# An RWKV-7 chunk scan: the outputs' score part multiplied by the inverse ahead of the scan, and the solve added into the output's bank

## The chip, the cores and the metric

The kernel runs on one core of a Trainium2 chip. Its metric is the device time of one execution in microseconds, the median over the runs shown. TensorE (PE) multiplies matrices, its weight loads are shown as an engine of their own (PEld); VectorE (DVE), ScalarE (ACT) and GpSimd (POOL) do the rest, and SyncE (SP) issues the transfers.

## The reference, cut to what matters

Two layers. Each normalizes x, projects it with one matrix, and feeds three mixers (pooling over windows, retention, RWKV-7); their gated outputs are projected, merged with sigmoid gates and projected once more. D_MODEL is 1024, the sequence 1024, a branch 512 wide. The change is in the third mixer, 8 heads of 64:

```python
def rwkv7_time_mix(p, shift_mu, w0, w2, a0, a2, k_k, k_a, r_k, ln_w, ln_b):
    ...
    xs = tuple(jnp.moveaxis(z, 1, 0) for z in (r_h, w_h, k_h, v_h, -kk, kk * a_h))

    def step(S, inp):
        r_t, w_t, k_t, v_t, a_t, b_t = inp
        sa = jnp.einsum('bhvk,bhk->bhv', S, a_t)
        S = (S * w_t[:, :, None, :] + sa[..., None] * b_t[:, :, None, :]
             + v_t[..., None] * k_t[:, :, None, :])
        return S, jnp.einsum('bhvk,bhk->bhv', S, r_t)

    _, y = lax.scan(step, jnp.zeros((B, H, N, N), jnp.float32), xs)
    y = jnp.moveaxis(y, 0, 1)
    y = head_norm(y, RWKV_NORM_EPS).reshape(B, T, BRANCH_W) * ln_w + ln_b
    ...
```

## The kernel before, in words

**Projections.** The large products run as three products of fp32r parts (`hi` by `hi`, `hi` by `lo`, `lo` by `hi`), 128x128 weights by 512 columns, into the banks `acc`. The weights come as `wr`; the scalar engine makes the high part `wh`, GpSimd the low part `wl`.

**RWKV by chunks.** The 1024 steps are 16 chunks of 64; two heads of 64 share the 128 partitions, so there are four head pairs (`hp`) a layer, one `rwkv_task` each, one after the other. A task prepares, for all 16 chunks, `AR` (decayed a and r), `BK` (decayed b and k), its transpose `BKt`, and the masked scores: the product burst `g` (64 rows by 128 columns, two heads in the two row halves) gives the triangular matrices that land in `Z` (a against b), `GQ` (r against b) and `KG` (both against k).

**The solve.** In a chunk, sa solves a triangular system; the kernel inverts the 64x64 unit triangular matrix of each chunk and head. The vector engine inverts the diagonal 32x32 blocks in `M` (a part of the tile `VB`) by 30 pairs of operations, and transposes move blocks between `Z`, `VB` and `G` (`STREAM_TRANSPOSE`). The 32x32 block below the diagonal takes two bursts of small products, `m1` and `m2` (both are named `m` in the profile), each 32 products of 32x32, four corners of the array in turn; the scalar and the vector engine empty their four banks (`mt<-m`, `G<-m`; the tiles `mn` and `mt` are W1 and W2). Then the whole inverse stands in `GQ` (columns 0 to 63), put together with two copies `G<-Z`.

**The scan.** For each chunk `c`, before the change, TensorE issues five products, each in float32 (two passes, so two MATMUL records): `cy<-VB,G` (values by scores, for the next chunk ahead of time, `own_values`), `cy<-S,AR` (state), `ch<-xst,G` (the inverse, applied to the right-hand side in `xst`), `ch<-Z,BKt` (the state update) and `cy<-xst,G` (the scores of the outputs, applied to the solution). Between them the vector engine copies the right-hand side into `xst` and the solution into `Z`, the scalar engine copies the solution into `xst`, and two operations make the new state `S`. Rows 64 to 127 of `cy` are the chunk's outputs, copied to `y`. The last chunk has no state update.

**Order.** The program is recorded first. `lanes` hold generators (tasks); each `yield` gives a delay on a virtual clock, and `pump` advances those that are due between projection products, so that tasks are woven into the projections. `plan_layer` says which weight tile comes next; while the RWKV tasks last it moves gate tiles ahead (written with `gd<-gsg`, read back with `gs<-gd`). Then `needs` finds the dependences, `cost` prices each instruction, and `weave` orders the instructions of each engine by a simulation with these prices: at each step the operation that can begin first, and among equals the one recorded with the earlier time. `bursts` are lists of products that wait together and run back to back. Each engine executes its list in order, so a wait holds up everything behind it. PSUM has three `acc` banks, two `mx`, two `cy` and one `ch`; bursts use `mx`, `cy`, `ch`, `cy`.

The planner's prices that the change or the prediction speaks of, before it:

```python
                o.load, o.occ, o.dur = (55, 53, 272) if k == 64 else (15, 15, 191)
...
            elif w == "transpose":
                d = 100 + 1.82 * n
...
            else:
                d, o.lock = 150 + 0.53 * n, True
```

The second is a transpose of the vector engine and the last its copy within SBUF, in ns for n columns; `lock` means that it holds a port that GpSimd's operations with `lock` also want.

Of the kernel before, what the change touches and what calls it, by code (L numbers as in the profile page):

```python
# [18 lines left out]
P = 128  # L19
# [241 lines left out]
class Prog:  # L261
# [50 lines left out]
    def needs(self):  # L312
# [6 lines left out]
        for chain in self.chains.values():  # L319
            old = []  # L320
            for b in chain:
                w, r, mine = [], [], []
                for o, m, write in uses[b]:
                    free = True
                    for q, x in w:
                        if x & m and q is not o:
                            o.pred[q.i] = "d"
                            free = False
                    if not write:
                        r.append((o, m))  # L330
# [12 lines left out]
                old = mine  # L343
# [10 lines left out]
    def cost(self, o):  # L354
# [6 lines left out]
        if o.eng == "PE":  # L361
            n = o.outs[0].free_size()
            rhs = o.ins[1]
            k = rhs.index.shape[0] * 32
            o.twice = rhs.dtype != F32R and w != "transpose"
            o.rows = k
            if rhs.dtype == F32R:
                o.load, o.occ, o.dur = (107, (n + 32) / 2.4, n / 2.4 + 176) if k == 128 else (55, 116, 393)
            elif k == 128:
                o.load, o.occ, o.dur = 109, 53, 273 if n > 1 else 250  # L370
            else:
                o.load, o.occ, o.dur = (55, 53, 272) if k == 64 else (15, 15, 191)
# [4 lines left out]
        if o.eng == "DVE":  # L377
            if w == "reciprocal":
                d = 140 + 6.2 * n
            elif w == "transpose":  # L380
                d = 100 + 1.82 * n
            elif w == "tensor_tensor_scan":
                d, o.lock = 150 + 1.7 * n, True
            elif w == "tensor_reduce":
# [29 lines left out]
    def weave(self):  # L414
# [25 lines left out]
        while len(order) < len(ops):  # L440
# [124 lines left out]
def trunk_kernel(ctx, tc, xT, cvec, pos, vecs, consts, w_ada, w_all, pool_w, lora_w, out):  # L565
# [47 lines left out]
    def cyt(s):  # L613
        return ps_c.tile([P, HF], F32, tag="cy", name=nm(s))
# [607 lines left out]
    def rwkv_task(l, hp, kT, rT, vp, lt, lw):  # L1222
# [169 lines left out]
        for i, (rows, hd, c8) in enumerate(quad[1:]):  # L1392
            (nc.scalar.copy, nc.vector.tensor_copy)[i % 2](
                q4(W1, rows, 1), GQ[0:32, c8, 32 * hd : 32 * hd + 32]
            )
        for b in (1, 0):
# [4 lines left out]
        for i, (rows, hd, c8) in enumerate(quad):  # L1401
            if i != 1:
                nc.scalar.copy(q4(W2, rows, 1), Z[32:64, c8, 64 * hd + 32 : 64 * hd + 64])
        place_values(1)

        def quads(name, lhsT, rhs):
            pss = [mx(name), cyt(name), cht(name), cyt(name)]
            at = len(nc.ops)
            for v in range(8):
                for g, (rows, hd, c8) in enumerate(quad):  # L1410
                    u, o = 2 * (c8.start + v) + hd, slice(32 * v, 32 * v + 32)
                    mmul(pss[g][rows, o], lhsT(g, rows, u, o), rhs(g, rows, u, o))
            nc.bursts.append((at, len(nc.ops)))
            return pss

        half2 = lambda t, rows, o: t[rows, 256 + o.start : 256 + o.stop]
        yield 1000
        yield wait(W1, G)
        pss = quads(
            "m1",  # L1420
            lambda g, rows, u, o: W1[rows, o] if g else N_[0:32, u, 32:64],
            lambda g, rows, u, o: half2(W1, rows, o) if g else t1(rows, u),
        )
# [6 lines left out]
        pss = quads(  # L1430
            "m2",
            lambda g, rows, u, o: W2[rows, o],
            lambda g, rows, u, o: half2(W2, rows, o) if g != 1 else N_[32:64, u, 32:64],
        )
        for g, (rows, hd, c8) in enumerate(quad):
            (nc.scalar.copy, nc.vector.tensor_copy)[g % 2](
                GQ[64 * hd : 64 * hd + 32, c8, 32:64], q4(pss[g], rows)
            )
        SS = [sp.tile([P, P], F32, tag="S", name=nm("S"), bufs=2) for _ in range(2)]
        for S in SS:  # L1440
            nc.gpsimd.memset(S, 0.0)
# [9 lines left out]
        for c in range(16):  # L1451
# [13 lines left out]
            if c < 15:  # L1465
                cy_next = own_values(c + 1)
            yield wait(xst)
            ch = cht("ch")
            mmul(ch[:, 0:P], GQ[:, c, :], xst)
            nc.vector.tensor_copy(Z[0:64, c, :], ch[0:64, 0:P])  # L1470
            for hd in range(2):
                cols = slice(64 * hd, 64 * hd + 64)
                nc.scalar.copy(xst[cols, cols], Z[0:64, c, cols])
            yield wait(Zt)
            if c < 15:
                mmul(ch[:, P : 2 * P], BKt[:, c, :], Z[:, c, :])
                for hd in range(2):
                    rw = slice(64 * hd, 64 * hd + 64)
                    cols = slice(P + 64 * hd, P + 64 * hd + 64)
                    if c:  # L1480
                        nc.vector.scalar_tensor_tensor(
                            Sn[rw, rw], ch[rw, cols], pc[rw, c : c + 1], SP[rw, rw], op0=ALU.mult, op1=ALU.add
                        )
                    else:
                        nc.vector.tensor_scalar_mul(Sn[rw, rw], ch[rw, cols], pc[rw, c : c + 1])
# [400 lines left out]
    for l in range(L):  # L1886
# [297 lines left out]
```

## Time and profile before

| what | value |
|---|---|
| median of 3 runs | 2299.82 us (2298.17 to 2301.0) |
| the profiled execution's own time | 2299.37 us |
| its span | 2297.6 us |
| mean granted clock of TensorE | 0.996 |
| busy: PE, DVE, ACT, POOL | 2249.1, 1470.3, 871.7, 821.2 us |
| products `acc<-hhi,wh`, `acc<-hlo,wh`, `acc<-hhi,wl` | 2000 each |

In the groups of instructions a row reads: line, engine, operation, what is written from what, shapes, count, then busy us and the mean ns of one, then the idle time of the engine just before them and what ended it. Every instruction has the same line (561), since one function issues them all; they are told apart by their tiles. In the timeline a row is start, duration (both us), engine and so on; `x32` means that many in a row, and a bracket holds the idle time before it with what ended that. Products are pipelined, so the difference of two starts, and not a duration, says how much of TensorE's time one takes. A row of stretches has from and to, the length, the busy time of TensorE with its count, the granted clock, the share of the transfer engines and GB/s.

### The profile page before, as it was taken

The page shows a single profiled execution, that of the slowest core. Times are in us where ns is not written, and L with a number is a line of the kernel's source. Part 1 is how long each engine was busy: PE and PEld are TensorE (multiplying, and loading weights), DVE is VectorE, ACT ScalarE, POOL GpSimd, SP SyncE. Part 2 cuts the span into 40 slices and gives each one's busy share as a digit, 9 for nine tenths or more (in the row PEclk, how much of TensorE's full clock was granted, in tenths as well). Part 3 has the DMA queues.
Part 4 walks back from the last instruction along what each step waited for, and adds up shares of the span by engine and source line. Part 5 has one row for each costly group of instructions (what it writes and reads, how often), then busy time and mean ns, then how long its engine had stood idle before and what let it go on. Part 6 is the DMA issues. An engine that isn't in the chain of part 4 may idle for free. (4 is left out here: it accounts for less than half of the span.)

```text
span 2297.6 us, 33901 instructions
## 1 busy us (share of the span) xinstructions
PE 2249.1 (98%) x12520; PEld 1879.9 (82%) x12520; DVE 1470.3 (64%) x2866; ACT 871.7 (38%) x1770; POOL 821.2 (36%) x714
## 2 busy tenths in 40 slices
PE   5999999999999999999999999999999999999998
PEld 4888888888888788887888888888878888788888
DVE  8677478587678754668547847866875784313644
ACT  5643442433443342223443334344344434212343
POOL 5222333233333342463442233323324333326441
PEclk9999999999999999999999999999999999999999
DMA  8132113112232225767431211311211222535442
GB/s 286 33 121 79 42 42 98 42 42 76 62 91 75 89 86 178 234 207 229 138 94 59 74 42 42 98 38 42 89 51 42 70 92 64 181 109 161 124 143 83
DMA packets 125942, 226.75 MB, mean 99 GB/s; under 512 B 14288, under 2 KB 17616, under 8 KB 125776
## 3 DMA queue, kind: packets, MB, share of 16 engines
q1 hardware_dynamic: 125776, 224.59, 31.7%
q8 instruction: 98, 1.61, 0.3%
q14 instruction: 68, 0.56, 0.1%
HBM read 176.03 MB, written 48.50 MB: 98 GB/s over the span
## 5 line engine op out<-in xcount | busy, mean ns | idle before, releaser
L561 POOL TENSOR_TENSOR wl<-wr,wh 128x512 fp32r<-128x512 f32 x342 | 458.2, 1340 | 1007.3 <-ACT wh L561 976.8
L561 PE MATMUL acc<-hhi,wh 128*128 128x512 f32 x2000 | 805.6, 403 | 0.8 <-DVE r L561 0.7
L561 PE MATMUL acc<-hlo,wh 128*128 128x512 f32 x2000 | 805.2, 403 | 0.0
L561 PE MATMUL acc<-hhi,wl 128*128 128x512 f32 x2000 | 801.6, 401 | 0.0
L561 ACT CAST wh<-wr 128x512 fp32r<-128x512 f32 x342 | 212.0, 620 | 621.6 <-PE acc L561 439.7
L561 PEld LDWEIGHTS acc<-hhi,wh 128*128 128x128 f32 x2000 | 377.5, 189 | 66.4 <-DVE r L561 1.4
L561 PEld LDWEIGHTS acc<-hlo,wh 128*128 128x128 f32 x2000 | 377.6, 189 | 64.2 <-issue 2.1
L561 PEld LDWEIGHTS acc<-hhi,wl 128*128 128x128 f32 x2000 | 377.5, 189 | 63.1
L561 PE MATMUL acc<-oG,wh 128*128 128x512 f32 x384 | 149.8, 390 | 0.0
L561 PE MATMUL acc<-oG,wl 128*128 128x512 f32 x384 | 149.7, 390 | 0.0
L561 PE MATMUL acc<-olo,wh 128*128 128x512 f32 x384 | 149.7, 390 | 0.0
L561 ACT COPY xst<-Z 64x64 f32<-64x64 f32 x256 | 62.4, 244 | 136.1 <-DVE Z L561 133.0
L561 DVE TENSOR_TENSOR VB<-VB,tm 64x30 f32<-64x30 f32 (+14 forms) x240 | 107.1, 446 | 7.0
L561 DVE SCALAR_TENSOR_TENSOR S<-ch,pc,SP 64x64 f32<-64x64 f32 x224 | 63.4, 283 | 68.9 <-PE ch L561 59.9
L561 DVE TENSOR_TENSOR tm<-VB 64x30 f32<-64x30 f32 (+14 forms) x240 | 97.6, 407 | 7.1
L561 DVE COPY xst<-cy 64x64 f32<-64x64 f32 x256 | 55.5, 217 | 72.7 <-PE cy L561 45.6
L561 DVE COPY Z<-ch 64x128 f32<-64x128 f32 x128 | 36.1, 282 | 92.4 <-PE ch L561 92.0
L561 ACT ACTIVATE gsg<-acc 128x512 f32<-128x512 f32 x86 | 51.2, 596 | 93.1 <-PE acc L561 63.0
L561 PEld LDWEIGHTS acc<-oG,wl 128*128 128x128 f32 x384 | 72.1, 188 | 15.0
L561 PEld LDWEIGHTS acc<-oG,wh 128*128 128x128 f32 x384 | 72.1, 188 | 14.9
L561 PEld LDWEIGHTS acc<-olo,wh 128*128 128x128 f32 x384 | 72.1, 188 | 14.8
L561 DVE SCALAR_TENSOR_TENSOR mrg<-gs,acc 128x512 f32<-128x512 f32 x32 | 21.9, 686 | 93.0 <-PE acc L561 93.0
(280 smaller groups left out, 3738.9 us busy)
## 6 DMA issues: line engine op xcount, KB each, us to landing
wr<-in_w_all SPq DMA_DIRECT2D x364, 256.0 KB, 2.7
gd<-gsg SPq DMA_DIRECT2D x86, 256.0 KB, 2.0
gs<-gd SPq DMA_DIRECT2D x86, 256.0 KB, 2.8
wada<-in_w_ada SPq DMA_DIRECT2D x70, 256.0 KB, 3.3
ol<-od SPq DMA_DIRECT2D x64, 256.0 KB, 3.6
ringG<-in_w_ada SPq DMA_DIRECT2D x26, 256.0 KB, 4.9
x<-in_xT SPq DMA_DIRECT2D x16, 256.0 KB, 5.0
od<-po SPq DMA_DIRECT2D x16, 256.0 KB, 2.1
```

The source lines that it names most:

```text
L561: f(*[put(x) for x in o.args], **{k: put(x) for k, x in o.kw.items()})
```

## The change

Ahead of the scan, the score matrix of the outputs is multiplied by the inverse for each chunk and head (burst `qt`, 32 products of 64x64 by 64 columns); the result takes the place of the scores in `GQ` (columns 64 to 127). To have the factor the right way round, `m2` is computed in both orders (the second half with the operands exchanged), another transpose `T2` of the diagonal blocks is made, and the blocks are laid out once for `qt` and once, less the identity, for the scan. The inverse less the identity is added to what already stands in the bank `cy`: one product `cy<-xst,G` now gives the solution (rows 0 to 63) and the finished outputs (rows 64 to 127). The product into `ch` with the inverse, and the scalar engine's copies of the solution into `xst`, are gone; `ch` is used for the state update alone.

Beside it: the planner's price of transposes (two values, by the number of dimensions of the output) and of small products; an order between readers of one PSUM buffer on different engines; a rule in `weave` that lets a ready GpSimd operation go first where a vector operation wants the same port within 50 ns; a fifth `mo` buffer; and the `post` tasks are drained with `rwkv` and `mix` before the branches are merged.

```diff
@@ needs
                     if not write:
+                        if b.space == PSUM:
+                            for q, x in r:
+                                if q.eng != o.eng:
+                                    o.pred.setdefault(q.i, "a")
                         r.append((o, m))
@@ cost
-                o.load, o.occ, o.dur = (55, 53, 272) if k == 64 else (15, 15, 191)
+                quad = k == 32 or o.ins[0].free_size() == 64
+                o.load, o.occ, o.dur = (15, 15, 191 if k == 32 else 230) if quad else (55, 53, 272)
...
-                d = 100 + 1.82 * n
+                d = (100 if len(o.outs[0].index.shape) == 3 else 300) + 1.88 * n
@@ weave
+            s = begin(o, f, lk)
+            if e == "DVE" and o.lock and ready["POOL"]:
+                g = free["POOL"]
+                lim = min(begin(x, g, 0.0) for x in ready["POOL"]) + 1e-6
+                x = min((x for x in ready["POOL"] if begin(x, g, 0.0) <= lim), key=lambda x: (x.prio, x.i))
+                if x.lock and lim < s + 50:
+                    o, e, q = x, "POOL", ready["POOL"]
+                    s = begin(o, g, lock["DVE"] - 100)
             q.remove(o)
-            s = begin(o, f, lk)
@@ trunk_kernel
-    t_mo = slot("mo", 4, HF + 16)
+    t_mo = slot("mo", 5, HF + 16)
...
-        drain("rwkv", "mix")
+        drain("rwkv", "mix", "post")
@@ rwkv_task, the solve
+        nc.vector.tensor_copy(q4(W1, quad[1][0], 1), GQ[0:32, 8:16, 0:32])
+        nc.scalar.copy(GQ[64:96, :, 0:32], GQ[0:32, :, 32:64])
+        nc.scalar.copy(q4(W1, quad[3][0], 1), GQ[0:32, 8:16, 32:64])
+        for rows in (slice(64, 96), slice(0, 32)):
+            nc.gpsimd.memset(GQ[rows, :, 32:64], 0.0)
...
+        T2 = VBt[32:64, 1024:2048]
+        nc.vector.transpose(
+            out=T2.rearrange("p (a b s) -> p s a b", s=32, b=2),
+            in_=M[32:64, :].rearrange("p (a b s) -> p s a b", s=32, b=2),
+        )
+        T2 = T2.rearrange("p (a b s) -> p a b s", s=32, b=2)
+        for hd in range(2):
+            nc.scalar.copy(GQ[64 * hd + 32 : 64 * hd + 64, :, 32:64], T2[:, :, hd, :])
+        back(0)
...
-        nc.scalar.copy(GQ[64:128, :, 0:64], Z[0:64, :, 64:128])
-        nc.vector.tensor_copy(GQ[0:64, :, 0:64], Z[0:64, :, 0:64])
...
+        for swap in range(2):
+            for g, rows, hd, c, o in units:
+                x, t2 = W2[rows, o], half2(W2, rows, o) if g != 1 else N_[32:64, 2 * c + hd, 32:64]
+                if swap:
+                    mmul(pss[g][rows, o], x, t2)
+                else:
+                    mmul(half2(pss[g], rows, o), t2, x)
+        nc.bursts.append((at, len(nc.ops)))
         for g, (rows, hd, c8) in enumerate(quad):
             (nc.scalar.copy, nc.vector.tensor_copy)[g % 2](
-                GQ[64 * hd : 64 * hd + 32, c8, 32:64], q4(pss[g], rows)
+                GQ[64 * hd + 32 : 64 * hd + 64, c8, 0:32], q4(pss[g], rows, 1)
             )
+        for g, (rows, hd, c8) in enumerate(quad):
+            (nc.scalar.copy, nc.vector.tensor_copy)[g % 2](
+                Z[0:32, c8, 64 * hd + 32 : 64 * hd + 64], q4(pss[g], rows)
+            )
+        yield 800
+        yield wait(G)
+        pss = [cht("qt"), cyt("qt")]
+        at = len(nc.ops)
+        for k in range(8):
+            for e in range(2):
+                for hd in range(2):
+                    rows = slice(64 * hd, 64 * hd + 64)
+                    mmul(
+                        pss[hd][64 * e : 64 * e + 64, 64 * k : 64 * k + 64],
+                        GQ[rows, 2 * k + e, 0:64], GQ[rows, 2 * k + e, 64:128],
+                    )
+        nc.bursts.append((at, len(nc.ops)))
+        eye = ident[0:64, 0:64].unsqueeze(1).to_broadcast([64, 16, 64])
+        for hd in range(2):
+            rows = slice(64 * hd, 64 * hd + 64)
+            nc.vector.tensor_tensor(GQ[rows, :, 0:64], Z[0:64, :, rows], eye, op=ALU.subtract)
+            for e in range(2):
+                nc.scalar.copy(
+                    GQ[rows, e:16:2, 64:128],
+                    pss[hd][64 * e : 64 * e + 64, :].rearrange("p (c n) -> p c n", n=64),
+                )
@@ rwkv_task, the scan
-            ch = cht("ch")
-            mmul(ch[:, 0:P], GQ[:, c, :], xst)
-            nc.vector.tensor_copy(Z[0:64, c, :], ch[0:64, 0:P])
-            for hd in range(2):
-                cols = slice(64 * hd, 64 * hd + 64)
-                nc.scalar.copy(xst[cols, cols], Z[0:64, c, cols])
-            yield wait(Zt)
+            mmul(cy[:, 0:P], GQ[:, c, :], xst, start=False, skip_group_check=True)
             if c < 15:
-                mmul(ch[:, P : 2 * P], BKt[:, c, :], Z[:, c, :])
+                nc.vector.tensor_copy(Z[0:64, c, :], cy[0:64, 0:P])
+            o = (c % 8) // 2 * P
+            nc.scalar.copy(y[64 * par : 64 * par + 64, o : o + P], cy[64:128, 0:P])
+            if c < 15:
+                yield wait(Zt)
+                ch = cht("ch")
+                mmul(ch[:, 0:P], BKt[:, c, :], Z[:, c, :])
...
-            yield wait(xst)
-            mmul(cy[:, 0:P], GQ[:, c, :], xst, start=False, skip_group_check=True)
-            o = (c % 8) // 2 * P
-            nc.scalar.copy(y[64 * par : 64 * par + 64, o : o + P], cy[64:128, 0:P])
             yield wait(Sn)
```

More of the change, by code (lines that the diff above doesn't have):

```diff
@@ L1391, in rwkv_task, with back @@
         )
[L1392 to L1396, printed above, removed]
+        nc.vector.tensor_copy(q4(W1, quad[1][0], 1), GQ[0:32, 8:16, 0:32])
[3 more added lines that the diff above has]
+            nc.gpsimd.memset(GQ[rows, :, 32:64], 0.0)
+        def back(b):
             q = slice(32 * b, 32 * b + 32)
@@ L1400, in rwkv_task @@
             )
-        for i, (rows, hd, c8) in enumerate(quad):
-            if i != 1:
+        back(1)
+        for rows, hd, c8 in quad:
+            if rows.start != 32:
                 nc.scalar.copy(q4(W2, rows, 1), Z[32:64, c8, 64 * hd + 32 : 64 * hd + 64])
-        place_values(1)
[L1406 to L1414, printed above, removed]
+        T2 = VBt[32:64, 1024:2048]
@@ L1416, in rwkv_task @@
+        nc.vector.transpose(
[6 more added lines that the diff above has]
+        back(0)
+        place_values(1)
         half2 = lambda t, rows, o: t[rows, 256 + o.start : 256 + o.stop]
+        units = [
+            (g, rows, hd, c8.start + v, slice(32 * v, 32 * v + 32))
+            for v in range(8) for g, (rows, hd, c8) in enumerate(quad)
+        ]
@@ L1417, in rwkv_task @@
         yield 1000
         yield wait(W1, G)
[L1419 to L1423, printed above, removed]
+        pss = [mx("m1"), cyt("m1"), cht("m1"), cyt("m1")]
+        at = len(nc.ops)
+        for g, rows, hd, c, o in units:
+            mmul(
+                pss[g][rows, o],
+                W1[rows, o] if g else N_[0:32, 2 * c + hd, 32:64],
+                half2(W1, rows, o) if g % 2 else GQ[rows, c, 0:32],
+            )
@@ L1424, in rwkv_task @@
+        nc.bursts.append((at, len(nc.ops)))
         for g, (rows, hd, c8) in enumerate(quad):
             (nc.scalar.copy, nc.vector.tensor_copy)[g % 2](W2[rows, 0:256], pss[g][rows, 0:256])
-        nc.scalar.copy(GQ[64:128, :, 0:64], Z[0:64, :, 64:128])
-        nc.vector.tensor_copy(GQ[0:64, :, 0:64], Z[0:64, :, 0:64])
         yield 800
         yield wait(W2)
[L1430 to L1434, printed above, removed]
+        pss = [mx("m2"), cyt("m2"), cht("m2"), cyt("m2")]
@@ L1435, in rwkv_task @@
+        at = len(nc.ops)
+        for swap in range(2):
+            for g, rows, hd, c, o in units:
+                x, t2 = W2[rows, o], half2(W2, rows, o) if g != 1 else N_[32:64, 2 * c + hd, 32:64]
[4 more added lines that the diff above has]
+        nc.bursts.append((at, len(nc.ops)))
         for g, (rows, hd, c8) in enumerate(quad):
             (nc.scalar.copy, nc.vector.tensor_copy)[g % 2](
-                GQ[64 * hd : 64 * hd + 32, c8, 32:64], q4(pss[g], rows)
+                GQ[64 * hd + 32 : 64 * hd + 64, c8, 0:32], q4(pss[g], rows, 1)
@@ L1438, in rwkv_task @@
             )
+        for g, (rows, hd, c8) in enumerate(quad):
[5 more added lines that the diff above has]
+        pss = [cht("qt"), cyt("qt")]
+        at = len(nc.ops)
+        for k in range(8):
+            for e in range(2):
+                for hd in range(2):
+                    rows = slice(64 * hd, 64 * hd + 64)
+                    mmul(
+                        pss[hd][64 * e : 64 * e + 64, 64 * k : 64 * k + 64],
+                        GQ[rows, 2 * k + e, 0:64], GQ[rows, 2 * k + e, 64:128],
+                    )
@@ new lines, in rwkv_task @@
+        nc.bursts.append((at, len(nc.ops)))
+        eye = ident[0:64, 0:64].unsqueeze(1).to_broadcast([64, 16, 64])
[6 more added lines that the diff above has]
+                    pss[hd][64 * e : 64 * e + 64, :].rearrange("p (c n) -> p c n", n=64),
+                )
@@ L1467, in rwkv_task @@
             yield wait(xst)
-            ch = cht("ch")
-            mmul(ch[:, 0:P], GQ[:, c, :], xst)
-            nc.vector.tensor_copy(Z[0:64, c, :], ch[0:64, 0:P])
-            for hd in range(2):
-                cols = slice(64 * hd, 64 * hd + 64)
-                nc.scalar.copy(xst[cols, cols], Z[0:64, c, cols])
-            yield wait(Zt)
-            if c < 15:
-                mmul(ch[:, P : 2 * P], BKt[:, c, :], Z[:, c, :])
+            mmul(cy[:, 0:P], GQ[:, c, :], xst, start=False, skip_group_check=True)
+            if c < 15:
+                nc.vector.tensor_copy(Z[0:64, c, :], cy[0:64, 0:P])
[5 more added lines that the diff above has]
+                mmul(ch[:, 0:P], BKt[:, c, :], Z[:, c, :])
                 for hd in range(2):
                     rw = slice(64 * hd, 64 * hd + 64)
-                    cols = slice(P + 64 * hd, P + 64 * hd + 64)
                     if c:
                         nc.vector.scalar_tensor_tensor(
-                            Sn[rw, rw], ch[rw, cols], pc[rw, c : c + 1], SP[rw, rw], op0=ALU.mult, op1=ALU.add
+                            Sn[rw, rw], ch[rw, rw], pc[rw, c : c + 1], SP[rw, rw], op0=ALU.mult, op1=ALU.add
                         )
                     else:
-                        nc.vector.tensor_scalar_mul(Sn[rw, rw], ch[rw, cols], pc[rw, c : c + 1])
+                        nc.vector.tensor_scalar_mul(Sn[rw, rw], ch[rw, rw], pc[rw, c : c + 1])
             yield 500
-            yield wait(xst)
-            mmul(cy[:, 0:P], GQ[:, c, :], xst, start=False, skip_group_check=True)
-            o = (c % 8) // 2 * P
-            nc.scalar.copy(y[64 * par : 64 * par + 64, o : o + P], cy[64:128, 0:P])
             yield wait(Sn)
```

## The prediction

> **What bounds the kernel now.** I read the page's shares and slices first, then the waits of TensorE's queue, then the timeline of TensorE inside one scan, one small burst and one wide burst. The profiled execution took 2299.37 us, 0.45 under the median of 2299.82; its span is 2297.6, so 1.8 us lie around it. The sums below are made in that execution and put on the median.
>
> ```profile
> span 2297.6 us, 33901 instructions
> PE 2249.1 (98%) x12520; PEld 1879.9 (82%) x12520; DVE 1470.3 (64%) x2866; ACT 871.7 (38%) x1770; POOL 821.2 (36%) x714
> PE   5999999999999999999999999999999999999998
> PEclk9999999999999999999999999999999999999999
> ...
> PE acc L561 <- DVE sq L561: 20.1, 3, 12.0
> PE cy L561 <- DVE G L561: 4.3, 3, 2.3
> ...
> PE rkv L561 <- ACT rkt L561: 2.5, 1, 2.5
> ...
> PE m L561 <- DVE mn L561: 1.4, 2, 0.7
> ```
>
> TensorE is busy in every slice but the first, at full clock; of its few waits 20.1 us belong to the start. Everything else has air (the vector engine 36%, the scalar engine 62%). So a product taken out of TensorE's queue moves the end by its whole place in that queue, and one put in costs its whole place. What a product takes is not its duration, since they are pipelined: it is read from starts.
>
> **The product removed.** Each chunk step of the scan now issues five products, the last of them `cy<-xst`, the second one with the matrix GQ and the state xst. The change folds it into the first.
>
> ```profile
> L561 PE MATMUL cy<-xst,G 128*128 128x128 f32 x256 | 49.3, 274 | 0.0
> ...
> 239.70 0.39 PE L561 MATMUL acc<-hhi,wh 128*128 128x512 f32 x1
> 239.93 0.39 PE L561 MATMUL acc<-hlo,wh 128*128 128x512 f32 x1
> 240.16 0.38 PE L561 MATMUL cy<-xst,G 128*128 128x128 f32 x2
> 240.30 0.47 PE L561 MATMUL acc<-hhi,wl 128*128 128x512 f32 x1
> 240.61 0.38 PE L561 MATMUL cy<-S,AR 128*128 128x128 f32 x2
> 240.75 0.48 PE L561 MATMUL acc<-hhi,wh 128*128 128x512 f32 x1
> 241.07 0.39 PE L561 MATMUL acc<-hlo,wh 128*128 128x512 f32 x1
> ```
>
> A float32 product is two passes, so 256 passes are 128 products (2 layers x 4 head pairs x 16 chunks). From 239.93 to 241.07 are 1.14 us: three projection products at 0.23 (239.70 to 239.93) and two scan products, so (1.14 - 0.69) / 2 = 0.225 us each. The 0.14 between 240.16 and 240.30 is only part of it, because the following projection product then takes 0.31 in place of 0.23. 128 x 0.225 = **-28.8 us**; the lower bound of the gain is 128 x 0.14 = 17.9. Nothing hides this and nothing takes its place: its neighbours are ready projection products.
>
> Off TensorE, 256 copies `xst<-Z` and the two big copies `G<-Z` go; of the removed `ch` only the bank changes. In the new step the scalar engine's copy of y follows the vector engine's copy of Z out of the same bank, 0.28 us later; the bank is wanted again two chunks later, so I count it nothing.
>
> **The products added.** The second 32x32 burst `m2` (64 passes) is doubled, and a new burst `qt` comes: 32 products of 64x64 by 64 columns, 64 passes, on four corners of the array in turn. Both are run once for each of the 8 head pairs and layers. No such 64x64 burst is in the trace; the nearest are the 32x32 burst and `g`, 64 rows by 128 columns.
>
> ```profile
> 401.45 0.39 PE L561 MATMUL acc<-hhi,wh 128*128 128x512 f32 x1
> 401.68 0.39 PE L561 MATMUL acc<-hlo,wh 128*128 128x512 f32 x1
> 402.00 0.21 PE L561 MATMUL m<-G,Z 32*32 32x32 f32 x1
> ...
> 402.53 0.23 PE L561 MATMUL m<-mn 32*32 32x32 f32 x4
> 402.68 0.50 PE L561 MATMUL acc<-hhi,wl 128*128 128x512 f32 x1
> 403.02 0.40 PE L561 MATMUL acc<-hhi,wh 128*128 128x512 f32 x1
> ...
> 495.51 0.40 PE L561 MATMUL acc<-hhi,wl 128*128 128x512 f32 x1
> 495.84 2.06 PE L561 MATMUL g<-AR,BK 64*128 64x128 f32 x32
> 497.82 0.50 PE L561 MATMUL acc<-hhi,wh 128*128 128x512 f32 x1
> 498.16 0.40 PE L561 MATMUL acc<-hlo,wh 128*128 128x512 f32 x1
> ```
>
> The 32x32 burst takes 403.02 - 401.68 - 2 x 0.23 = 0.88 us of the queue, about 0.55 of them for the 64 passes (402.00 to just past 402.53) and 0.33 for going in and out. Doubling it inside one burst costs 0.55 each: 8 x 0.55 = **+4.4 us**; as a burst of its own it would be 8 x 0.88 = 7.0.
>
> For `qt` the ends are these. If its four corners run beside each other as the four of the 32x32 burst do, a pass has twice the columns and costs twice as much: 64 passes at 1.1 us, with the 0.33 about 1.43: 8 x 1.43 = 11.4. If only the two row halves run beside each other, as in `g`, its 64 passes of half the columns cost what 32 passes of `g` do, 498.16 - 495.51 - 0.46 = 2.19: 8 x 2.19 = 17.5. I take **+11.4**, because qt, like the 32x32 burst, goes to corners that share neither all rows nor all columns, and keep 17.5 as a rival.
>
> Here two pages of the Trainium skill disagree. "TensorEngine Tiling (Array Packing)", Key Properties, has tiles of the array load weights and multiply independently, 64x64 being four such tiles; "TensorE: Matmul & The Clock Gate", The mechanism, lets a weight load overlap running products only when the group of rows differs. By the first the sum stays at 11.4, by the second it is 17.5; both fit the bursts of this trace, whose neighbours always differ in rows, so the trace does not decide.
>
> **The solve's other engines, and its waits.** After m2 the kernel today waits for two copies on the vector engine.
>
> ```profile
> L561 DVE STREAM_TRANSPOSE Z<-VB 32x1024 f32<-32x1024 f32 x16 | 32.1, 2004 | 0.5
> L561 DVE STREAM_TRANSPOSE G<-VB 32x1024 f32<-32x1024 f32 x8 | 17.7, 2218 | 0.3
> L561 DVE COPY G<-m 32x256 f32<-32x256 f32 x16 | 6.8, 422 | 2.5 <-PE m L561 1.4 <-ACT G L561 0.7
> L561 ACT COPY BKt<-bt 128x512 f32<-128x512 f32 x32 | 18.8, 587 | 23.6 <-PE bt L561 23.2
> ...
> 777.19 1.63 DVE L561 COPY G<-Z 64x1024 f32<-64x1024 f32 x1
> 777.22 2.52 POOL L561 TENSOR_TENSOR pt<-pt 128x525 f32<-128x525 f32 x2
> 779.63 0.87 DVE L561 COPY G<-m 32x256 f32<-32x256 f32 x2
> 780.20 1.19 PE L561 MATMUL cy<-VB,G 128*128 128x128 f32 x4 [2.28 <-DVE G L561]
> 781.04 0.77 PE L561 MATMUL acc<-hhi,wh 128*128 128x512 f32 x1
> ...
> 591.94 0.86 PE L561 MATMUL cy<-VB,G 128*128 128x128 f32 x4 [1.69 <-DVE G L561]
> ...
> 774.50:787.00 12.50, 10.13 (x159) 0.73 0.25 86
> ```
>
> `G<-Z` ran 1.63 us beside a GpSimd operation, where the planner has 150 + 0.53 x 1024 = 693 ns. Behind it stood the copies that empty the two banks the scan's first product needs, and TensorE, in order, stood 2.28 us there and 1.69 in another task. After the first of these the clock fell: 0.73 over 12.5 us, products at 0.77 in place of 0.39 for some 5 us, about 2.4 us more. The change drops this copy: -(2.28 + 1.69 + 2.4) = -6.4. In place of it come two more places where TensorE waits in order with all projection products queued behind it: qt for the copies of m2 (four on each engine in place of two), and the scan's second product for qt's. The wait `PE m <- DVE mn` shows such places at 0.7 us in 2 of 8 tasks; I put 8 x 0.36 = +2.9 for them. Net **-3.5**, ends -6.4 and +7 (0.9 in every task). The planner's corrected price of a transpose (100 + 1.82 x 1024 = 1964 before, 2218 in the row) works the same way and is inside that term.
>
> The solve gets longer too: one more transpose (2.0), two more rounds of emptying (0.42 each), qt (1.4), four copies of 512 columns by the scalar engine (4 x 0.59, as `BKt`), less the old copy (0.9): about 5.7 us a task. The vector engine's subtractions run beside qt's copies. Projection products cover this; what if they do not is a rival below.
>
> **Edits counted at nothing.** The fifth `mo` slot: the one wait for a slot that reaches TensorE is the 2.5 us at `rkv`, so 0 to -2.5. Draining the post tasks with the others records the last transposes and the write `od<-wob` of a layer ahead of the `ol`, `gs` and weight loads on SyncE's queue; TensorE has a whole third branch of ready products there. Taking GpSimd first on a tie delays a vector operation by at most one weight split; 36% of the vector engine is free. The wait between two readers of one bank is in the trace already, so planning it only orders work: 0 to 0.6 at the start. Together -3 to +2.
>
> ```profile
> 19.32 0.59 ACT L561 COPY rbs<-rbc 128x512 f32<-128x512 f32 x1 [1.09 <-DVE x L561]
> 19.94 1.88 DVE L561 TENSOR_TENSOR x<-x,rbc 128x512 f32<-128x512 f32 x3 [0.58 <-ACT rbs L561]
> ...
> L561 SPq DMA_DIRECT2D gd<-gsg x86: 319/326/423, 128.0 to 2009.9; - x86
> ```
>
> **Sum.** -28.8 + 4.4 + 11.4 - 3.5 = -16.5 us: 2299.8 - 16.5 = **2283.3 us**.
>
> **Rivals.** *Two corners at a time.* qt costs 17.5: -10.4, **2289.4**. For it speaks that the two column halves read weights through the same rows; against it, nothing here.
>
> *New waits eat the gain.* Every task gets a wait like the one at 780.20: 2.28 and 2.4 of slow clock. One such task in three (8 x 4.7 / 3 = 12.5, in place of -3.5) leaves -0.5: **2299**. For it: a longer chain with more in-order waits; against it: the copies out of PSUM kept their price in the trace (422 in the mean), and only the copy that ran beside GpSimd missed.
>
> *The filling work runs out* (slower). The longer solve must be covered by gate tiles moved ahead; 86 writes `gd<-gsg` are 43 of the 48 tiles, so 5 are left, each 48 products x 0.23 = 11 us, 55 in all, against 8 x 5.7 = 46 needed. If the chain of one layer is uncovered at its end, TensorE idles 4 x 5.7 = 23: -16.5 + 23 = +6.5, **2306**; it decides from 21 us of new idle time on. Against it: after the branches merge, products of the first two branches are ready.
>
> *The scan's product filled a hole*, so that its removal saves nothing: then +12, 2312. The full TensorE slices speak against it.
>
> **Chances.** Forecast (2272 to 2287) 0.50, two corners (2284 to 2294) 0.34, waits 0.09, filling 0.05, hole 0.02. The range 2272 to 2297 goes from qt at its low end with all waits gone and the slot's 2.5 us to the case with qt at 17.5, m2 as a burst of its own and the waits at their middle. A change of 0.2% (4.6 us) is about what a measurement of this kernel can tell from none. Faster by that: 0.87 (both first cases and part of the third); within: 0.07; slower: 0.06.
>
> **What would show it.** `cy<-xst` at 256 passes and `ch<-xst` gone; a qt group of 512 passes whose burst takes 1.4 us (right) or 2.2 (two corners) between its neighbours; m2 at 1.4; no wait of `cy` for `G` near 2 us; TensorE's waits outside the start no larger than now. The forecast is wrong if TensorE shows new idle stretches at the solves or at the layer's end, or if the clock falls there.

## The result, and the profile after

| kernel | median, us | against the kernel before, with its 95% interval |
|---|---|---|
| before, in the same comparison | 2298.99 | 1 |
| after (4 runs, 2275.24 to 2277.27) | 2276.12 | 0.9904 [0.9892, 0.9916] |

The change saves 22.9 us. 2283.3 was forecast: the sign is right, the time lies in the range, and the gain is larger than the 16.5 us of the sum. The profiled execution took 2275.24 us, with a span of 2273.4.

The page after, its span and busy times:

```profile
span 2273.4 us, 35182 instructions
PE 2229.2 (98%) x13288; PEld 1863.2 (82%) x13288; DVE 1491.3 (66%) x2890; ACT 842.6 (37%) x1570; POOL 830.7 (37%) x730
```

TensorE has 768 more records (512 of `qt` and 512 of the doubled `m2`, less 256 of the product taken out) and 19.9 us less busy time; it is still the bound. Now the waits of its queue (total us, times, longest):

```profile
PE acc L573 <- DVE sq L573: 16.8, 3, 11.8
PE acc L573 <- DVE hlo L573: 4.0, 1, 4.0
PE acc L573 <- ACT hhi L573: 2.7, 1, 2.7
...
PE m L573 <- issue: 0.3, 1, 0.3
PE qt L573 <- DVE Z L573: 0.3, 1, 0.3
```

The wait of `cy` for `G` (4.3 us before) and that of `rkv` (2.5) are gone. Of the two new in-order places, `qt` waits 0.3 us and the scan's second product, `cy<-xst`, not at all. The groups of the scan and of the small bursts:

```profile
L573 PE MATMUL cy<-VB,G 128*128 128x128 f32 x256 | 49.8, 276 | 0.0
L573 PE MATMUL cy<-xst,G 128*128 128x128 f32 x256 | 49.4, 274 | 0.0
L573 PE MATMUL cy<-S,AR 128*128 128x128 f32 x240 | 46.1, 273 | 0.0
L573 PE MATMUL ch<-Z,BKt 128*128 128x128 f32 x240 | 45.9, 272 | 0.0
...
L573 PE MATMUL qt<-G 64*64 64x64 f32 x512 | 10.6, 222 | 0.4 <-DVE Z L573 0.3
L573 PE MATMUL m<-mt 32*32 32x32 f32 x768 | 10.5, 193 | 0.3 <-issue 0.3
```

Four products a chunk step are left, in 16 steps of 8 tasks, and no line `ch<-xst`. How long the new burst holds the queue is read from its neighbours' starts, as in the prediction (timeline of TensorE):

```profile
1695.53 0.40 PE L573 MATMUL acc<-hlo,wh 128*128 128x512 f32 x1
1695.86 1.16 PE L573 MATMUL qt<-G 64*64 64x64 f32 x64
1696.95 0.50 PE L573 MATMUL acc<-hhi,wl 128*128 128x512 f32 x1
1697.29 0.39 PE L573 MATMUL acc<-hhi,wh 128*128 128x512 f32 x1
```

1697.29 - 1695.53 - 2 x 0.23 = 1.30 us: the four corners do run side by side (1.43 forecast, 2.19 for two at a time). Three of the eight bursts are unbroken like this one, 0.94 us from the first start to the last; the other five have breaks of 0.2 to 0.6 us, 1.7 in all.

The solves are where idle time went. Rows of stretches, one for each of the eight, from 1 us ahead of `m1` to 2 us past the second scan product; of before all, with the sum:

```profile
209.70:218.70 9.00, 8.98 (x164) 1.00 0.34 113
401.00:409.70 8.70, 8.38 (x162) 1.00 0.25 82
585.80:595.10 9.30, 7.61 (x156) 1.00 0.27 86
773.80:784.00 10.20, 7.83 (x150) 0.76 0.29 101
1313.40:1323.40 10.00, 9.55 (x165) 1.00 0.19 49
1502.30:1513.40 11.10, 9.83 (x166) 1.00 0.10 27
1689.70:1700.70 11.00, 9.72 (x166) 1.00 0.08 25
1876.90:1885.50 8.60, 8.60 (x163) 1.00 0.19 63
sum 77.90, PE 70.50; mean PE 8.81
```

and of after, the two with most work in them and the sum:

```profile
805.30:823.20 17.90, 17.64 (x322) 1.00 0.11 35
...
1684.00:1702.30 18.30, 17.16 (x320) 1.00 0.11 30
...
sum 126.60, PE 124.65; mean PE 15.58
```

The mean length goes from 77.90 / 8 = 9.7 to 126.60 / 8 = 15.8 us, +6.1 (5.7 forecast), and all of it is covered: 126.60 - 124.65 = 2.0 us idle in all eight, where before it was 7.4, with another 0.24 x 10.20 = 2.5 lost to the clock of 0.76.

For every run below I split the span in the same way. Idle is the span less TensorE's busy time; slow clock is the sum of (1 - granted clock) over the records of the clock; work is the rest.

| run | profiled span | idle | slow clock | work | idle and slow clock at the 8 solves |
|---|---|---|---|---|---|
| before | 2297.6 | 48.5 | 10.0 | 2239.1 | 7.4, 2.5 |
| after | 2273.4 | 44.2 | 2.5 | 2226.7 | 2.0, 0 |
| after again | 2276.1 | 45.5 | 5.8 | 2224.9 | 3.0, 0 |
| planner edits only | 2292.3 | 45.6 | 7.4 | 2239.2 | 7.3, 3.4 |
| products only | 2281.6 | 48.2 | 6.5 | 2226.9 | 6.5, 1.7 |
| and transposes' price | 2278.3 | 44.9 | 8.1 | 2225.3 | 3.0, 3.4 |
| fifth product back | 2299.8 | 44.1 | 6.3 | 2249.4 | 1.1, 0 |
| `qt` twice | 2283.9 | 46.5 | 5.1 | 2232.4 | 5.2, 0 |
| copy on the scalar engine | 2298.3 | 47.7 | 9.8 | 2240.8 | 7.2, 2.6 |
| `qt` column halves one after the other | 2280.1 | 45.8 | 5.7 | 2228.6 | 2.3, 0 |
| no reader order | 2286.0 | 53.6 | 9.3 | 2223.1 | 2.0, 0 |
| no GpSimd-first | 2271.8 | 41.9 | 6.1 | 2223.7 | 1.3, 0 |
| four `mo` slots | 2278.5 | 46.5 | 7.8 | 2224.2 | 4.3, 3.4 |
| `qt` row halves one after the other | 2269.8 | 39.0 | 3.4 | 2227.5 | 1.6, 0 |

In the profiled executions 24.2 us of span are 12.4 of work, 4.3 of idle time and 7.5 of slow clock. Seven runs have the new products in their own order; their work is 2223.1 to 2226.9, 2225.0 in the mean, and of the three with the old products 2239.7. So the products are worth 14.7 us, give or take 2, and waits and clock bring the rest. The split counts some time twice: at the very end of every run the clock is halved while TensorE mostly stands idle. Counted only while TensorE is busy, the slow clock is 6.0 us before and none after, and the work of the two groups of runs still differs by 14.9. The clock's part is also partly the luck of an execution: half-clock stretches at the start stand in some executions of one kernel and not in others (after has none there, after again loses 1.7 us by one).

### The profile page after: what moved, and what is told of

Same layout as the page of the kernel before. It is cut to its first block, busy times and chain, and to the rows that moved or that the text cites. A ratio compares the mean times of both kernels' runs of the same rounds, so it can differ in the third digit from the quotient of the medians.

```text
span 2273.4 us, 35182 instructions
## 1 busy us (share of the span) xinstructions
PE 2229.2 (98%) x13288; PEld 1863.2 (82%) x13288; DVE 1491.3 (66%) x2890; ACT 842.6 (37%) x1570; POOL 830.7 (37%) x730
## 4 chain that ended last, share of the span: by engine, by line
PE 68%; DVE 3%; POOL 1%; DMA 1%; issue 1%; ACT 0%; DVEq 0%; SPq 0%; POOLq 0%; ACTq 0%
PE acc L573 58%; PE cy L573 3%; PE ch L573 1%; PE g L573 1%; PE ro L573 1%; PE rkv L573 0%; PE rs L573 0%; DVE VB L573 0%; PE bt L573 0%; PE m L573 0%; DVE Z L573 0%; PE lw L573 0%; PE pps L573 0%; DMA ol<-od 0%; POOL olo L573 0%
## 5 line engine op out<-in xcount | busy, mean ns | idle before, releaser
L573 DVE COPY Z<-cy 64x128 f32<-64x128 f32 x120 | 33.8, 281 | 81.3 <-PE cy L573 80.8
L573 ACT ACTIVATE SP<-S,pc 128x128 f32<-128x128 f32 x120 | 48.2, 402 | 101.0 <-DVE S L573 100.8
L573 ACT COPY y<-cy 64x128 f32<-64x128 f32 x128 | 33.5, 262 | 140.4 <-DVE Z L573 132.1
L573 PEld LDWEIGHTS acc<-oG,wl 128*128 128x128 f32 x384 | 72.1, 188 | 14.7
```

Of the source, the lines that this page charges most:

```text
L573: f(*[put(x) for x in o.args], **{k: put(x) for k, x in o.kw.items()})
```

## The experiments

Three comparisons, each with its own runs of the kernel before (2298.45, 2297.15 and 2297.44 us).

### What the parts are worth apart

**The planner's edits on the old products.** The kernel before with the price of transposes and small products, the reader order, GpSimd-first, `mo` of 5 and the longer drain:

```diff
-                d = 100 + 1.82 * n
+                d = (100 if len(o.outs[0].index.shape) == 3 else 300) + 1.88 * n
...
+                        if b.space == PSUM:
+                            for q, x in r:
+                                if q.eng != o.eng:
+                                    o.pred.setdefault(q.i, "a")
...
-    t_mo = slot("mo", 4, HF + 16)
+    t_mo = slot("mo", 5, HF + 16)
...
-        drain("rwkv", "mix")
+        drain("rwkv", "mix", "post")
```

> The kernel before with the change's edits to the planner, the fifth mo buffer and the draining of post, but the five products as they were. Theory P (the products themselves and the copy that goes with them made the gain): the big copy G<-Z on the vector engine keeps its too low price, so the two waits of about 2 us for the scan's first banks stay; only the waits inside m1 (0.9 twice) and the one at rkv (2.4) may go: 2294 to 2298 us. Theory O (the 6 us beyond the forecast came from the better order): 2290 to 2293 us.

Measured: 2293.75 us, ratio 0.9982 [0.9972, 0.9991], -4.7 us, between the two ranges. The solves keep their idle time. Rows of stretches of the third and the fourth:

```profile
586.90:601.00 14.10, 10.78 (x161) 0.76 0.21 76
780.30:789.30 9.00, 6.67 (x151) 1.00 0.24 79
```

But these are no longer the waits of before. The copy `G<-Z` of the vector engine takes 0.68 to 0.81 us in all eight tasks here, where before it took 1.63 at these two solves and 0.69 at the other six, and the wait of `cy` for the vector engine's `G` has fallen from 4.3 to 0.9:

```profile
PE m L573 <- DVE mn L573: 1.7, 2, 1.5
...
PE cy L573 <- DVE G L573: 0.9, 2, 0.5
```

In its place `m1` waits 1.5 us for `mn` and a product `pps` 1.3 us at the third solve, where the clock falls; at the fourth, `cy` waits 1.0 for the scalar engine's part of `G` and `ch` 1.4 for `xst`. So these edits are worth something without the products; they end the old wait and do not clear the solves.

**The products on the old plan.** The kernel after with the same edits taken back (the drain and the price of small products stay):

```diff
-                        if b.space == PSUM:
-                            for q, x in r:
-                                if q.eng != o.eng:
-                                    o.pred.setdefault(q.i, "a")
...
-                d = (100 if len(o.outs[0].index.shape) == 3 else 300) + 1.88 * n
+                d = 100 + 1.82 * n
...
-            if e == "DVE" and o.lock and ready["POOL"]:
...
-    t_mo = slot("mo", 5, HF + 16)
+    t_mo = slot("mo", 4, HF + 16)
```

> The changed kernel with the planner's old transpose price, without the order between readers of a bank, without the rule that lets GpSimd go first, and with four mo buffers; the new products, their price and the draining of post stay. Theory P: 2276 to 2280 us. Theory O: 2281 to 2284 us.

Measured: 2288.12 us, 0.9954 [0.9937, 0.997], above both ranges and 12 us above after. The profiled execution, at 2283.39, was its lowest, so the trace shows only 8.2 of the 12: 4.0 of idle time and 4.0 of slow clock. Its work is that of after (2226.9). The wait of `cy` for `G` is gone, since the copy is; new waits of TensorE's queue stand in its place:

```profile
PE m L562 <- DVE mn L562: 1.9, 1, 1.9
PE qt L562 <- ACT Z L562: 1.6, 1, 1.6
...
PE qt L562 <- DVE Z L562: 0.8, 1, 0.8
```

`qt` is the first of the two in-order places that the prediction had priced. The second, `cy<-xst`, shows no wait in this run or in any other with the new products; `m` for `mn` is a wait inside the old part of the solve.

Products alone -10.3, edits alone -4.7, both -21.0 to -22.9: 6 to 8 us exist only where both are, give or take 5 by the intervals of the three. That speaks for the theory that the plan carries a part of the gain, against the one that gives it all to products and copy.

**The price of transposes put back.** The run before this one with the one line of the price as in after:

```diff
-                d = 100 + 1.82 * n
+                d = (100 if len(o.outs[0].index.shape) == 3 else 300) + 1.88 * n
```

> The kernel of e2_products_only with the corrected price of the vector engine's transposes put back, nothing else. Theory T: the waits inside m1, m2 and qt, which that kernel showed (6 us in all), go: 2278 to 2281 us. If the other planner edits (order of readers, GpSimd first, fifth buffer) carry it: it stays at 2285 to 2288 us.

Measured: 2284.72 us, 0.9938 [0.9923, 0.9953]: 3.4 of the 12 us, with overlapping intervals. The waits of `m` for `mn` are gone, those of `qt` stay at 1.6 and 0.7. At the fourth solve TensorE still runs dry and the clock falls, in the rows of stretches:

```profile
812.20:830.20 18.00, 15.55 (x301) 0.81 0.13 40
```

18.00 - 15.55 = 2.4 idle and 0.19 x 18 = 3.4 by the clock. In this plan no projection product stands between `m2` and `qt` there.

**No reader order.** The kernel after without the four lines in `needs`:

```diff
-                        if b.space == PSUM:
-                            for q, x in r:
-                                if q.eng != o.eng:
-                                    o.pred.setdefault(q.i, "a")
```

> The changed kernel without the order between readers of one bank in the planner (the chip waits there in any case). Of 8.6 us that e7_price_too is slower than the changed kernel, three edits can be the cause. Theory R (this one: two engines now read cy in each of 128 chunk steps, and a plan that does not know of the wait puts the products that follow too early): 2281 to 2285 us, with waits of TensorE or slow clock at the solve near 815 us. Otherwise 2275 to 2278 us.

Measured: 2285.94 us, 0.995 [0.9935, 0.9964], 9.8 us above after. Not at the solves (2.0 idle, as in after): most is lost in the first 100 us. Rows of stretches of this run,

```profile
0.00:100.00 100.00, 66.65 (x283) 0.97 0.51 175
```

and of after.

```profile
0.00:100.00 100.00, 73.10 (x311) 1.00 0.50 175
```

6.45 us more idle time and 3 us of slow clock. The waits of this run name the places, where after has 2.7 and 4.0 us:

```profile
PE acc L569 <- ACT hhi L569: 6.5, 2, 4.9
...
PE acc L569 <- DVE hlo L569: 5.3, 1, 5.3
```

All that differs between the two kernels is whether the planned order knows that readers of one bank on different engines wait for each other. That knowledge alone doesn't decide: three other plans are without it and lose no such time in this stretch. Before has 73.02 us busy there, products only 72.61, and with the price of transposes put back it is this row:

```profile
0.00:100.00 100.00, 72.40 (x312) 0.98 0.51 175
```

That kernel differs from this one by GpSimd-first and the fifth slot. So the loss at the start belongs to a plan that has these two without the reader order, and which of them it takes is open. The slow clock of this stretch (0.97) is no sign of the edit: before has as much there.

**No GpSimd-first.** The kernel after without the eight lines in `weave`:

```diff
-            if e == "DVE" and o.lock and ready["POOL"]:
...
-                    o, e, q = x, "POOL", ready["POOL"]
-                    s = begin(o, g, lock["DVE"] - 100)
```

> The changed kernel without the rule that lets GpSimd go first. Theory G (this rule keeps the low parts of the weights ahead, so that projection products are ready between m2 and qt): 2281 to 2285 us. Otherwise 2275 to 2278 us.

Measured: 2273.67 us, 0.99 [0.9884, 0.9917], so not slower than after, and the theory of this rule has failed: in this plan the edit brings nothing.

**Four `mo` slots.** The kernel after with:

```diff
-    t_mo = slot("mo", 5, HF + 16)
+    t_mo = slot("mo", 4, HF + 16)
```

> The changed kernel with four mo buffers. Theory B (the fifth buffer frees the retention tasks that share the time of the solves, and the rkv product near the end): 2279 to 2284 us, with the wait of rkv back. Otherwise 2275 to 2278 us.

Measured: 2281.66 us, 0.9933 [0.9918, 0.9948], +5.5. The wait at `rkv`, which the prediction tied to the slot, did not come back. The fourth solve stalled, in the waits of TensorE's queue:

```profile
PE qt L573 <- ACT Z L573: 1.6, 1, 1.6
```

This stall is tied to the slot. It stands at the fourth solve, with 1.6 us, in all three runs with the new products and four slots (this one, products only, and with the transposes' price) and in none of the eight with five. These three are also the only runs with the new products in which the clock falls at a solve (the table's last column). Here four projection products stand between `m1` and `m2` of that solve and none between `m2` and `qt`; after has 17 and 8 there. The idle 2.5 us and the 3.4 of slow clock of that solve are the size of the 5.5. How a slot for another stage's tile frees these products was not followed further.

The longer drain and the price of small products were not taken back in any run; their share isn't known.

### The prices of the products

**The fifth product back.** The kernel after with a product of the old size put in a part of the bank `ch` that nobody reads, in 15 of 16 chunk steps (the outputs don't change):

```diff
                 mmul(ch[:, 0:P], BKt[:, c, :], Z[:, c, :])
+                mmul(ch[:, P : 2 * P], GQ[:, c, :], xst)
```

> The changed kernel with a fifth product in each of 15 chunk steps (the inverse and scores by xst into unused columns of ch, result not used): 120 products. By the place read from starts (0.225 us each): +27 us, 2303 us. By the 0.14 us between its start and the next one: +17, 2293 us. If it fills holes: under +5, 2281 us.

```profile
L573 PE MATMUL ch<-xst,G 128*128 128x128 f32 x240 | 46.0, 273 | 0.0
```

Measured: 2301.7 us, 1.0015 [1.0006, 1.0024], 25.6 above after. The group has 240 passes, 120 products: 25.6 / 120 = 0.213 us each, or (2249.4 - 2225.0) / 120 = 0.203 by the work. The timeline gave 0.225 and the row's duration would give 0.55 for two passes. 128 products are then 26 to 27 us, not a hole that was free anyway.

**`qt` computed twice.** All 32 products of the burst issued again in it:

```diff
+        for again in range(2):
             for k in range(8):
```

> The changed kernel with the 32 products of qt issued twice in one burst. Four corners beside each other: about 64 passes in 0.96 us more, 8 times, +7.7 us: 2284 us. Two corners at a time (64 passes in 1.8 us): +14 us: 2290 us.

Measured: 2289.4 us, 0.9956 [0.9941, 0.9971], +13.3; its profiled execution is 3.7 below that. The work rose by 2232.4 - 2225.0 = 7.4, which is 8 x 0.94, what 64 further passes take from start to start in a burst without a break. The rest is not in the passes: the solves idle 5.2 us in place of 2.0, and two of its bursts have a break of over 1 us inside, for which the trace shows no semaphore. So the doubled burst shows the price of the passes only in the trace, not in the time.

**The order of the corners.** In after neighbours alternate between the two row halves (`hd`), then the column halves (`e`). First with the column halves one after the other:

```diff
-        for k in range(8):
-            for e in range(2):
+        for e in range(2):
+            for k in range(8):
                 for hd in range(2):
```

> The changed kernel with the 32 products of qt in another order: first all that write the lower 64 rows of their banks, then all that write the upper ones, so that neighbours are two corners that differ in rows and never four. If the four corners load and multiply independently and TensorE takes what lies next in its queue: a burst goes from 1.3 to about 2.1 us, +6 us on the mark of this set. If only the difference in rows counts, as the one rule says: no change.

Its burst in the timeline:

```profile
1701.03 0.40 PE L573 MATMUL acc<-hlo,wh 128*128 128x512 f32 x1
1701.36 1.91 PE L573 MATMUL qt<-G 64*64 64x64 f32 x64
1703.20 0.50 PE L573 MATMUL acc<-hhi,wl 128*128 128x512 f32 x1
1703.53 0.39 PE L573 MATMUL acc<-hhi,wh 128*128 128x512 f32 x1
```

Measured: 2281.24 us, 0.9927 [0.9912, 0.9941], +5.1. The burst holds the queue 1703.53 - 1701.03 - 0.46 = 2.04 us in place of 1.30: 8 x 0.74 = 5.9. This is close to the 2.19 that the rival of two corners had. (The row half also picks the bank that is written, so rows and banks change together here.)

Then with the row halves one after the other:

```diff
-        for k in range(8):
-            for e in range(2):
-                for hd in range(2):
+        for hd in range(2):
+            for k in range(8):
+                for e in range(2):
```

> The changed kernel with qt in the order: all products on the lower 64 rows of the array, then all on the upper, so that neighbours share their rows and differ only in the columns they write. If corners are independent whatever they share: like e8_qt_col_outer, 1.7 us a burst and 2281 us. If weight loads overlap only where rows differ: 64 loads one after the other, 3.4 us a burst and about 20 us more, 2295 us.

```profile
1692.77 0.39 PE L573 MATMUL acc<-hlo,wh 128*128 128x512 f32 x1
1693.09 1.91 PE L573 MATMUL qt<-G 64*64 64x64 f32 x64
1694.93 0.49 PE L573 MATMUL cy<-VB,G 128*128 128x128 f32 x2
```

Measured: 2271.74 us, 0.989 [0.9875, 0.9905], below both expected times. The burst is as long as with the columns apart: 1.91 in both. The starts of single passes show how: with two corners, in either order, two passes start 6 to 7 ns apart and the next two 58 ns after the first; in after four start within 20 ns, and the next four again 58 ns after the first. So a corner takes a pass about every 58 ns, and what counts is how many corners take turns.

Yet this is the lowest time of all runs: idle 39.0 us where after and after again have 44.2 and 45.5, and no wait above 0.5 us at `m`, `qt` or the scan. Its interval overlaps after's, so it is not shown to be better. Summed from first to last start, its eight bursts take 13.5 us and after's 9.3, since none here has a break; so bursts that are 4.3 us longer in all can come with a plan that waits 5 to 6 us less.

**The kernel after again,** unchanged, in the second comparison:

> The changed kernel once more, unedited, as the mark for the other runs of this set: 2276 us. If the chip itself takes 4 us more or less than in the first measurement, this run shows it.

Measured: 2276.11 us, 0.9901 [0.9884, 0.9917]. Times of two comparisons can be set side by side to one or two microseconds.

### The copy that the prediction blamed

**The big copy on the scalar engine.** The kernel before, the copy `G<-Z` that ran 1.63 us beside GpSimd moved off the vector engine:

```diff
-        nc.vector.tensor_copy(GQ[0:64, :, 0:64], Z[0:64, :, 0:64])
+        nc.scalar.copy(GQ[0:64, :, 0:64], Z[0:64, :, 0:64])
```

> The kernel before with one edit: the big copy G<-Z after m1 goes to the scalar engine instead of the vector engine. Theory C (this copy beside a GpSimd operation made the two waits of about 2 us and the slow clock after one of them): no wait of cy for G near 2 us, 6 us less, about 2292 us. Theory T (the waits come from the transposes' price): the waits stay somewhere in the solves, 2296 to 2299 us.

Measured: 2299.7 us, 1.001 [1.0, 1.0019]: nothing gained. Its waits and the two rows of stretches of the solves at which the copy had stood:

```profile
PE cy L561 <- DVE G L561: 4.2, 7, 1.1
```

```profile
584.50:594.30 9.80, 8.15 (x154) 0.91 0.35 131
774.20:783.80 9.60, 7.86 (x150) 0.82 0.28 105
```

The same wait has 4.2 us in all, in seven pieces in place of three, and the clock falls at two solves in place of one. But this edit doesn't take the copy out of the chain. The copies `G<-m` that empty the banks write into blocks that `G<-Z` has filled, so they follow it on either engine. The scalar engine now makes both `G<-Z` one after the other in 2.11 us, and the vector engine's copies wait for it, in the timeline of the two engines:

```profile
777.74 2.11 ACT L561 COPY G<-Z 64x1024 f32<-64x1024 f32 x2
...
778.82 0.43 DVE L561 COPY G<-m 32x256 f32<-32x256 f32 x1 [0.54 <-ACT G L561]
779.89 0.42 DVE L561 COPY G<-m 32x256 f32<-32x256 f32 x1 [0.64 <-ACT G L561]
```

So this run shows that moving the copy to another engine doesn't help; it does not show that the copy had no part in the wait. Two runs above say more on that: where the vector engine's copy took 0.7 us (planner edits only) the wait for it fell to 0.9, and where the copy was dropped (products only) it was gone.

## Why the prediction was right, and where it was not

**The products: right.** Forecast -28.8 + 4.4 + 11.4 = -13.0, measured -14.7 of work, give or take 2. By parts: a removed product is 0.20 to 0.21 us in place of 0.225 (26 to 27 us); the doubled `m2` takes 0.53 us more in bursts without a break, 8 x 0.53 = 4.2; `qt` is 8 x 1.30 = 10.4, with its breaks 12.1. These parts add up to -10 to -13, at or just under the low end of the measured work. The method of the prediction, starts of the neighbours, held in every case in which it was tried.

**The four corners: right.** In after the corners come in turn over both halves, and the burst holds the queue for 1.30 us. With the row halves one after the other, neighbours share their rows and differ in columns only; the burst took 1.91, to the hundredth what it took with neighbours of other rows, and the passes of two such neighbours start 6 ns apart. So a difference in columns serves as well as one in rows, and both together are best. The Trainium skill, "TensorE: Matmul & The Clock Gate", The mechanism, says that a weight load overlaps running products only when the group of rows differs. The trace does not bear this out here. The Trainium skill, "TensorEngine Tiling (Array Packing)", Key Properties, has different tiles load weights and multiply in parallel, and with this the trace agrees.

**The waits: the mis-sized term.** Forecast -3.5, measured -7 to -12 (idle -4.3 and clock -7.5 in the one profile, -3.0 and -4.2 in the other); at the solves alone -7.9 and -6.9. Three steps of it:

- The -6.4 for the copy. The wait that the prediction tied to the copy, `cy` for `G`, did go wherever the copy was dropped, and the idle time and slow clock of those two solves came out at its size: 1.69 + 2.37 idle and 2.5 of clock at 585.8 and 773.8 before, 0.4 idle after. The step took for granted that nothing stands behind that wait. With the planner's edits alone 3.3 and 2.3 us idle stay at these two solves; with the products alone the third is clear, the fourth idles 2.6 us, at `qt`, and the second, which had 0.3 before, idles 2.6 too, at `m1`. Only the products and the plan together clear them all.
- The +2.9 for the two new in-order waits did not come: 0.3 us at `qt`, none at `cy<-xst`. But it was no fancy: with the products alone `qt` waits 1.6 and 0.8.
- "Edits counted at nothing", -3 to +2 together, is the step that failed most. With the new products, the four edits taken back together cost 12 us. Taken out of after one at a time, the reader order costs 9.8, the fifth slot 5.5 and GpSimd-first nothing; the transposes' price, put back into the products alone, brings 3.4, which is not clear of the scatter. They don't add up. The slot was priced by a wait of the kernel before (`rkv`, 2.5); what it is worth in the new kernel is the stall at the fourth solve, which the kernel before could not show.

So the products on the old plan gave 10.3 at the median and 16.0 in the profiled execution, the lowest of four; the sum was 16.5. The plan gave the rest. At the median the products alone fall 6 us short of the sum and the whole change goes 6 us beyond it. That the time came out inside the range, near its low end, owes something to luck, since what the plan was worth stood in no term.

**The rivals.** Two corners: refuted by 1.30 us. New waits: 0.3 us where 12.5 was priced; with four slots one such task does stand, with 2.5 us idle and 3.4 of slow clock. Filling work: 88 writes `gd<-gsg` after, 86 before, so one tile of 48 more was moved ahead, not the five that were left; the solves, with 2.0 us idle in all, are covered by other products. The hole: refuted by the fifth product, +25.6.

**What stays open.** Why this plan meets the solves so well isn't settled. Each small edit reorders everything behind it, and the runs with the same products scatter from 2271.8 to 2286.0 in span. For the slot the stall that it ends is shown; for the reader order only that this plan needs it, and for the row order of `qt` only that the plan became another one. Of the breaks inside `qt` in five of after's eight bursts, one holds the wait for `Z` of 0.3 us; the others have no cause in the trace.

## What to carry to other kernels

Price a product by the starts of its neighbours, not by its duration, and check the price by adding the product back in an unread place: 0.225 read, 0.20 to 0.21 measured, where durations said 0.55. Where an engine runs in a planned order, split both spans into idle time, slow clock and work before explaining anything: here the work was forecast to about 2 us while waits, which any edit of the plan moves, swung by 5 to 12. To test a long operation that stands in front of a wait, take it out of the chain: on another engine the copy `G<-Z` still stood ahead of the same waits. And look for what waits right behind it, for that is what is left when it is gone.

## What the runs showed of the hardware

- 64 float32 passes of 64x64x64 go from first to last start in 0.94 us with all four corners in turn (15 ns a pass), and in 1.69 (27 ns) with two corners, whether these share their columns or their rows.
- In these bursts a corner of 64x64 took one pass about every 58 ns, whether two corners took turns or four.
- The vector engine's copy `G<-Z` of 64x1024 took 0.69 us in six tasks of before and 1.63 in the two in which it ran beside GpSimd's `pt<-pt`. The scalar engine's copy of the same size took 1.04 in all eight, beside GpSimd or not.
- Idle time at a solve comes with slow clock in some cases and not in others: 2.4 us idle came with 2.5 and 3.4 of slow clock at 773.80 before and at 812.20 with the transposes' price, while 2.3 at 780.30 with the planner's edits only came with none, and neither did 1.1 at 1684.00 in after. The runs show no length of wait that decides it.
